# Tokens' 1/rms spread by four fp32r products with a constant square, and four weight remainders moved from GpSimd to VectorE

## The chip, the cores and the metric

The kernel runs on one core of a Trainium2 chip. The metric is the device time of one execution in microseconds, as the median of several runs. TensorE (PE) multiplies, VectorE (DVE), ScalarE (ACT) and GpSimd (POOL) work on vectors, SyncE (SP) issues most transfers.

## What is computed

One decoder layer on 1024 tokens of width 1024, in float32. Cut to what matters here:

```python
h = rmsnorm(x, norm_g) * (1 + scale) + shift      # 1/rms of every token
u = h @ w_in                                      # 40 tiles of 128 columns
cv, cg, cs, lx, ls = split(u)
v = causal_depthwise_conv(cv * sigmoid(cg))       # 31 taps
y_conv = (silu(layernorm(v)) @ pw2 + b) * silu(cs)
hs = linear_scan(a, bx)                           # from lx, gates r and i
y = concat(y_conv, hs * silu(ls)) @ w_out
out = rmsnorm(x + (1 + gate) * y, final_g)
```

`rmsnorm` multiplies by `rsqrt(mean(x * x) + 1e-6)`; `shift`, `scale` and `gate` are products of `silu(c)` with `mod_w`.

## The kernel before

Channels lie on the partitions, the 1024 tokens along the free axis, so a tile is 128x1024, and products are made in halves of 512 tokens. A float32 product is made of three products in fp32r: each operand is split into a rounded part (`hi`, a cast by ScalarE) and the remainder (`lo`, a subtraction, `SUB` at L382), and hi x hi, lo x hi and hi x lo are summed in PSUM. Three such products in a row are called a triple below.

All instructions are put into one list by a planner (`Plan`, L120). Every operation has an engine, an assumed cost, a priority (lower goes first) and the buffers that it reads and writes; `Plan.order` runs the five engines in a model of time, and an engine that is free takes the ready operation of lowest priority. What comes out is a fixed order for each engine, and each engine then executes its own order strictly. So any number in the table of constants can move instructions far from the place that it names.

The kernel begins with four tiles of `w_in`, `FIRST` (L32): for every group k of 128 channels, x is scaled by `gs` and split (`uh`, `ul`), and their products are summed in seven banks of PSUM (`first`, `fw_mm`, L796). The eighth half has no bank and is made afterwards (`late`, L1340). These products do not yet hold 1/rms or shift: 1/rms, one value per token and the same on all partitions (`rbc`), is multiplied in when they leave PSUM (`first_u`, L1336 and L1344), and the share of shift is added as a bias. That bias is a product of `shift` with the weights: `fsum` collects it on VectorE (L973 to L1006), and the product `psbias` (L1009) sums it over the partitions. The three tiles of `NEXT` (numbers 4, 5 and 6) are made in the same way, from number 7 on the finished input h is used, which takes the place of `uh` and `ul` (`inputs`, L1026).

The statistics for 1/rms: ScalarE squares x, VectorE sums the squares of the eight groups into `sq` (L933 to L943), so that 128 partial sums per token are left. Eight products with a column of ones (L949) put the sums of 128 tokens each into columns of the bank `psb`; root and reciprocal work on 128x8 values (`st`); one product turns them into 8 rows of 128 (`turn`, L959); these are copied out, written to DRAM and read back on all 128 partitions (L962 to L966). `psb` is also the name `token_stats` in the profile.

The remainders `lo` of the weights are made by GpSimd for the tiles with a number below `EARLY` = 11, and by VectorE from there on (`weights`, L494). `p_prep` is the priority of cast and remainder. `conv_tile` makes the 31 taps; for three of the tiles, with partial sums that GpSimd's queue adds by DMA. All convolutions are summed in `csum`, whose mean over the channels is a product with the constant square `minus_r` (-1/1024 everywhere, L440), and so is the sum of squares behind it (`root_by_ones`, L1277): a cast, a remainder, two products for each half, and then a reciprocal root with one Newton step. This is the same construction that the change uses for 1/rms.

Of the kernel before, what the change touches and what calls it, by code (L numbers as in the profile page):

```python
# [9 lines left out]
F32 = mybir.dt.float32  # L10
# [4 lines left out]
P = 128  # L15
# [69 lines left out]
GLO = 'DVE'  # L85
GDOT = 'DVE'
FOLD = 'DVE'
EARLY = 11
ISSUE, FLIGHT, RATE = 1.0, 10.0, 3.0
GM = 14  # L90
TAPP = 15
TP = -60
SCALE = ("DVE", "DVE", "DVE", "DVE", "DVE", "DVE", "DVE", "DVE")
SQP, RSP, BIP, HHP, HCH, EVP = -84, -110, -50, -56, 0.1, -80
RBC_LAG = 2.0
FIRSTCOST, EARLYRATE, SQD, SQK, ULS = {-99: 1.7, -98: 0.9, -97: 1.0, -96: 1.6}, 410e3, 1, 1, 1.2


# [21 lines left out]
class Plan:  # L120
# [14 lines left out]
    @staticmethod  # L135
    def keys(items):
        for it in items:
            if isinstance(it, tuple):
                yield it
            else:  # L140
                for i in range(it.parts):
                    yield (it, i)
# [162 lines left out]
def hymba_layer(ctx: ExitStack, tc: tile.TileContext, xT, xa, vecs, mod_w, mod_s0, w_first, w_pairs, w_in,  # L305
# [76 lines left out]
    def SUB(prio, eng, lo, full, hi, n=T, r=(), w=(), reserve=0):  # L382
        return TT(prio, eng, lo, full, lambda: hi().bitcast(F32), ALU.subtract, n, r, w, reserve)
# [8 lines left out]
    def DMA(prio, out, in_, nbytes, r=(), w=(), after=(), reserve=0):  # L392
        cost = max(0.1, nbytes / (EARLYRATE if prio < -94.5 + KT * 3.3 else 360e3))
        cost = FIRSTCOST.get(round(prio), cost) if prio < -94 else cost
        return S.op("SP", cost, lambda: sp.dma_start(out(), in_()), prio, r, w, after=after,
                    reserve=reserve)
# [7 lines left out]
    def big_buf(name, dt=F32, parts=1):  # L404
        return S.buf("big", name, dt, parts)
# [39 lines left out]
    def ctile(name, n):  # L445
        return const.tile([P, n], F32, tag=name, name=name)
# [30 lines left out]
    def w_slice(s, k, nk, p_load, p_prep, first_load=(), eng="POOL", late=()):  # L477
        n, c = nk * P, slice(k, k + nk)
        keys = lambda b: [(b, i) for i in range(k, k + nk)]
        rw, hi, lo = raw[s], whi[s], wlo[s]  # L480
        cut = lambda b: (lambda: k3(b)()[:, c, :])
        DMA(p_load, cut(rw), lambda: wsrc(s)[:, c, :], n * P * 4, w=keys(rw), after=first_load)
        ACT(p_prep, cut(hi), cut(rw), "copy", n, r=keys(rw), w=keys(hi), after=late)
        SUB(p_prep, eng, cut(lo), cut(rw), cut(hi), n, r=keys(rw) + keys(hi), w=keys(lo))

    def w_bufs(s, where=None):
        n = number[s]
# [5 lines left out]

    def weights(s, after=(), n=None, eng=None, where=None, late=()):  # L494
        n = number[s] if n is None else n
        eng = eng or ("POOL" if n < EARLY else "DVE")
        w_bufs(s, where)
        w_slice(s, 0, KT, n - 2.5, n - 1.4, after, eng, late)

# [20 lines left out]
    def half(b, i):  # L520
        return part(b, i * H, i * H + H)
# [224 lines left out]
    cs, ps_c = ctile("cs", KT), [bank(f"c_row{z}") for z in range(len(CPARTS))]  # L746
    ps_g, cd = bank("scale0"), CPARTS[-1][0]
    ACT(-130, lambda: cs, lambda: V[:, OFF["c"]:OFF["c"] + KT], AF.Silu, KT, w=[("cs", 0)])
    ACT(-101, lambda: junk, lambda: eps_t, AF.Sqrt, 1, r=[("cs", 0)], w=[("junk", 0)])

    def idle_mm():
        pe.matmul(psb()[:, :P], ones, ones, start=True, stop=True)
# [180 lines left out]
    sqs = []  # L933
    for k in range(KT):
        p = SQP + k
        sq = big_buf(f"sq{k}")
        ACT(p, sq, xt[k], AF.Square, r=[xt[k]], w=[sq], after=[scaled[k]])
        if k:
            to = sqs[0]
            TT(p, SUM[k], to, to, sq, ALU.add, r=[to, sq], w=[to],  # L940
               after=[last_split[k + SQD]] if k <= SQK else [])
        else:
            sqs.append(sq)  # L943
    rbc = big_buf("rbc", parts=4)
    st, wk = ctile("st", KT), [psb]

    def stats(sq, k):
        for b in range(KT):
            pe.matmul(psb()[:, b:b + 1], sq()[:, b * P:b * P + P], ones[:, 0:1],  # L949
                      start=k == 0 and b == 0, stop=k == len(sqs) - 1, skip_group_check=True)  # L950

    for k, sq in enumerate(sqs):
        S.op("PE", 0.23 * KT, lambda sq=sq, k=k: stats(sq, k), RSP, [sq], wk, columns=4 * P * KT,
             after=[last_u[LASTK - 1, 3, 0]] if k else [])
    root = ACT(RSP, lambda: st, lambda: psb()[:, :KT], AF.Sqrt, KT, bias=eps_t,
               scale=1.0 / D, r=wk, w=[("st", 0)])
    S.op("DVE", 0.2, lambda: dve.reciprocal(st, st), RSP, [("st", 0)], [("st", 0)])

    def turn():  # L959
        pe.matmul(psb()[:KT, P:2 * P], st, ident, start=True, stop=True)  # L960
    spread = S.op("PE", 0.2, turn, RSP, [("st", 0)], wk, columns=4 * P)
    row, flat = lambda: rbc()[:KT, :P], dram.tile([KT, P], F32, tag="rrow", name="rrowd")  # L962
    spread_out = ACT(RSP, row, lambda: psb()[:KT, P:2 * P], "copy", P, r=wk, w=[(rbc, 0)])
    S.op("ACT", 0.3, lambda: act.dma_start(flat, row()), RSP, [(rbc, 0)], [("rrowd", 0)], lag=0.1)
    DMA(RSP, rbc, lambda: flat.rearrange("b p -> (b p)").partition_broadcast(P), FULL_BYTES,
        r=[("rrowd", 0)], w=[rbc])  # L966


    fsum, bias = big_buf("fsum", parts=2), ctile("bias", len(FIRST + NEXT))
    facc = part(fsum, 0, FW)  # L970
    for s in NEXT:
        weights(s, where="all", late=[root if s == NEXT[0] else spread_out])
    for k in range(KT):  # L973
        p = due[f"h{k}"]
        a_ = col(macc, k)
# [87 lines left out]
    def apart(b, a, e):  # L1063
        return lambda: b().rearrange("p (q m) -> p q m", q=2)[:, :, a // 2:e // 2]
# [262 lines left out]
    for i, (s, ps) in enumerate(zip(FIRST, psf)):  # L1327
        j, p, bi = s[1] % KT, EVP + i, bias[:, i:i + 1]
        t = big_buf(f"first_u{i}", parts=4)
        for a, e in START:  # L1330
            tk, pk, n = halves(t, a, e), halves(ps, a, e), e - a
            if (a, e) in cuts[i]:
                alone = len(cuts[i]) == 1
                if alone:
                    ACT(RSP, part(t, a, e), part(ps, a, e), "copy", n, r=pk, w=tk)
                TT(p - 4 * alone, "DVE", part(t, a, e), part(t if alone else ps, a, e),  # L1336
                   part(rbc, a, e), ALU.mult, n, r=(tk if alone else pk) + halves(rbc, a, e),
                   w=tk).slack = RBC_LAG
            else:
                late = bank("late")  # L1340
                for k in range(KT):
                    fw_mm(RSP + 60 + 0.1 * k, late, i, uhs[k], uls[k], k, ((a, e),),
                          after=[spread], off=a)
                TT(p, "DVE", part(t, a, e), part(late, 0, n), part(rbc, a, e), ALU.mult, n,  # L1344
                   r=[late] + halves(rbc, a, e), w=tk)
            if s[1] < CG:
                if a == 0:
                    v[j] = big_buf(f"v{j}")
                STT(p + 3, apart(v[j], a, e), by_two(t, a, e), bi, by_two(sig[j], a, e), ALU.add,
                    ALU.mult, n, r=tk + halves(sig[j], a, e) + [("bias", 0)], w=[v[j]])  # L1350
        if s[1] >= CG:
            ACT(p + 3, t, t, AF.Sigmoid, bias=bi, r=[t, ("bias", 0)], w=[t])
            sig[j] = t
# [303 lines left out]
```

## Time and profile before

| | |
|---|---|
| median of 3 runs | 727.97 us (727.45 to 728.03) |
| profiled execution: its time, its span | 727.49 us, 725.5 us |
| granted TensorE clock | 0.998 |
| HBM | 107 GB/s over the span |
| GpSimd's remainders `wlo<-raw,whi` | 7, of 2.39 to 3.38 us |
| VectorE's remainders of the same shape | 39, 1.22 us each |
| loads of a ScalarE table | 47, 1.28 us each |

The span goes from the first to the last instruction. A group's row in the profile names the line of the source, the engine, the operation, the tile written and the tiles read. Lines are those of the kernel before; in the changed kernel the same lines stand one or two further down.

### The profile page before, as it was taken

What the parts mean: (1) busy time and instruction counts of PE and PEld (TensorE: products, weight loads), DVE (VectorE), ACT (ScalarE), POOL (GpSimd) and SP (SyncE); (2) the same over time, 40 slices, a digit from 0 to 9 for tenths busy, and PEclk for the clock granted to TensorE, in tenths of its full rate; (3) what the DMA queues carried; (4) which work ended last, traced back from release to release, by engine and by line L of the source; (5) the groups of instructions that cost most, each with busy time, mean ns of one, the idle gap of its engine ahead of it and who ended that gap; (6) DMA issues with size and microseconds to landing.
All of it is one profiled execution on the core that took longest, in us unless ns stands there. A gap on an engine that the chain in (4) does not pass through costs nothing.

```text
span 725.5 us, 8895 instructions
## 1 busy us (share of the span) xinstructions
PE 717.6 (99%) x3250; PEld 597.2 (82%) x3250; DVE 634.4 (87%) x898; ACT 469.9 (65%) x653; POOL 97.5 (13%) x105
## 2 busy tenths in 40 slices
PE   9999999999999999999999999999999999999996
PEld 7888888888888888888888888888888888888886
DVE  6978999999989987787899995998999766997757
ACT  7663766777877878947758885835764334645443
POOL 0042013121232332232021100000000000000001
PEclk9999999999999999999999999999999999999999
DMA  8971026588699799698784545243332530434216
GB/s 334 407 265 63 1 94 136 137 190 190 144 254 239 152 222 221 144 204 169 175 172 101 111 88 161 88 174 134 127 117 77 212 116 2 159 111 137 60 57 232
DMA packets 36634, 112.10 MB, mean 155 GB/s; under 512 B 4072, under 2 KB 10992, under 8 KB 36592
## 3 DMA queue, kind: packets, MB, share of 16 engines
q1 hardware_dynamic: 23760, 76.89, 29.8%
q0 software_dynamic: 12528, 34.26, 26.2%
q8 instruction: 25, 0.41, 0.2%
q10 hardware_dynamic: 304, 0.40, 0.2%
q14 instruction: 17, 0.14, 0.1%
HBM read 64.69 MB, written 12.59 MB: 107 GB/s over the span
## 4 chain that ended last, share of the span: by engine, by line
PE 99%; DVE 0%; ACT 0%; DVEq 0%; issue 0%
PE ps L506 66%; PE first L805 5%; PE pbpw L617 3%; PE pupw L617 3%; PE papw L617 3%; PE gate L1246 3%; PE out L687 2%; PE puout L617 2%; PE paout L617 2%; PE pcpw L617 1%; PE pb0out L617 1%; PE pcout L617 1%; PE late L805 1%; PE out6b L687 1%; PE c_row L757 0%; PE pb1out L617 0%
## 5 line engine op out<-in xcount | busy, mean ns | idle before, releaser
L506 PE MATMUL ps<-uh,whi 128*128 128x512 f32 x576 | 224.2, 389 | 0.0
L506 PE MATMUL ps<-ul,whi 128*128 128x512 f32 x576 | 224.2, 389 | 0.0
L506 PE MATMUL ps<-uh,wlo 128*128 128x512 f32 x576 | 224.2, 389 | 0.0
L506 PEld LDWEIGHTS ps<-uh,wlo 128*128 128x128 f32 x576 | 108.1, 188 | 22.5
L506 PEld LDWEIGHTS ps<-ul,whi 128*128 128x128 f32 x576 | 108.1, 188 | 22.4
L506 PEld LDWEIGHTS ps<-uh,whi 128*128 128x128 f32 x576 | 108.1, 188 | 22.3
L347 ACT CAST whi<-raw 128x1024 fp32r<-128x1024 f32 x46 | 47.9, 1046 | 35.7 <-PE ps L506 30.4
L355 ACT ACT_TABLE_LOAD x47 | 60.3, 1283 | 5.5 <-PE ps L506 3.4
L374 DVE TENSOR_TENSOR wlo<-raw,whi 128x1024 fp32r<-128x1024 f32 x39 | 47.5, 1218 | 17.2 <-ACT whi L347 17.1
L379 POOL DMA_DIRECT2D es<-cq x45 | 39.6, 894 | 152.5 <-ACT cq L355 84.9
L366 DVE SCALAR_TENSOR_TENSOR cacc<-v,V,cacc 128x511 f32<-128x511 f32 (+14 forms) x75 | 55.5, 740 | 0.5
L366 DVE SCALAR_TENSOR_TENSOR caccs<-v,V,caccs 128x511 f32<-128x511 f32 (+6 forms) x70 | 52.1, 744 | 1.4
L366 DVE SCALAR_TENSOR_TENSOR caccs<-c,wsum,caccs 128x511 f32<-128x511 f32 (+6 forms) x70 | 51.9, 741 | 0.6
L379 POOL DMA_DIRECT2D oo<-co x42 | 39.9, 949 | 90.9 <-ACT co L355 61.3
L506 PE MATMUL ps<-yh,wlo 128*128 128x512 f32 x128 | 49.8, 389 | 0.0
L506 PE MATMUL ps<-yh,whi 128*128 128x512 f32 x128 | 49.8, 389 | 0.0
L506 PE MATMUL ps<-yl,whi 128*128 128x512 f32 x128 | 49.8, 389 | 0.0
L374 POOL TENSOR_TENSOR fg<-fg,bc 128x512 f32<-128x512 f32 x2 | 2.5, 1280 | 281.5 <-ACT bc L347 281.5
L366 DVE SCALAR_TENSOR_TENSOR xs<-ps,V,xs 128x512 f32<-128x512 f32 (+3 forms) x48 | 35.7, 743 | 0.2
L355 ACT ACTIVATE cq<-v,V 128x511 f32<-128x511 f32 (+14 forms) x45 | 31.7, 710 | 0.0
L366 DVE SCALAR_TENSOR_TENSOR modw<-modw,sc 128x1024 f32<-128x1024 f32 x23 | 30.1, 1313 | 0.4 <-DMA modw<-in_mod_w_dram 0.4
L355 ACT ACTIVATE cq<-c,wsum 128x512 f32<-128x512 f32 x42 | 29.9, 714 | 0.0
(385 smaller groups left out, 1444.7 us busy)
## 6 DMA issues: line engine op xcount, KB each, us to landing
raw<-in_w_in_dram SPq DMA_DIRECT2D x36, 512.0 KB, 5.2
modw<-in_mod_w_dram SPq DMA_DIRECT2D x23, 512.0 KB, 9.1
raw<-in_w_out_dram SPq DMA_DIRECT2D x10, 512.0 KB, 3.6
scsd<-scs SPq DMA_DIRECT2D x8, 512.0 KB, 3.8
acc<-in_xT_dram SPq DMA_DIRECT2D x8, 512.0 KB, 4.6
accd<-acc SPq DMA_DIRECT2D x8, 512.0 KB, 2.6
rawpw<-in_pw_dram SPq DMA_DIRECT2D x8, 512.0 KB, 3.3
scsr<-scsd SPq DMA_DIRECT2D x8, 512.0 KB, 6.1
```

Source lines behind the costliest of these rows:

```text
L347: act.copy(out(), in_())
L355: act.activation(out=out(), in_=in_(), func=func, **kw)
L366: dve.scalar_tensor_tensor(out=out(), in0=in0(), scalar=scalar, in1=in1(), op0=op0, op1=op1, accum_out=accum)
L374: lambda: e.tensor_tensor(out=out(), in0=a(), in1=b(), op=op), prio, r, w,
L379: return S.op("POOL", ISSUE, lambda: pool.dma_start(out(), a(), accum_op=ALU.add), prio, r, w, lag=RATE * n / T, after=after)
L506: pe.matmul(part(ps, a - off, b - off)(), k3(lhs)()[:, k, :], rhs[k]()[:, a:b], start=(k == 0 and lhs is wh and rhs is xh and (a - off) % ...
L617: pe.matmul(part(ps, 0, c1 - c0)(), half(*lhs)()[:, j * P:j * P + P], half(*rhs)()[:, c0:c1], start=start and j == 0 and z == 0, stop=j == ...
L687: pe.matmul(part(ps, a - off, e - off)(), k3(lhs)()[:, k, :], rhs()[:, i * H + a % H:i * H + a % H + e - a], start=k == KORD[0] and lhs is ...
L805: pe.matmul(part(ps, a - off, b - off)(), fw_part(lhs, k, i * P, i * P + P)(), rhs()[:, a:b], start=k == 0 and lhs is wh and rhs is xh, st ...
L1246: pe.matmul(ps(), lhs()[:, j, :], rhs()[:, c0:c1], start=st == 0, stop=st == 2)
```

## The change

The statistics are made in another way, in two halves of 512 tokens. ScalarE rounds the sum of squares to fp32r and VectorE takes the remainder (`sqhl`); two products with `minus_r` leave the negative mean of squares of every token on all 128 partitions; ScalarE copies it out of PSUM. Then ScalarE takes the reciprocal root (`Abs_reciprocal_sqrt`) and half of its square (`sqq`), and VectorE makes a Newton step of two operations that ends in `rbc`. The products with ones, the turning product, the reciprocal on 128x8 and the way over DRAM go. The table that ScalarE loads at the start is that of the reciprocal root.

The remainders of the weights with the numbers 4 to 7 are made by VectorE, each at a priority of its own (`LOP`). The casts of the `NEXT` weights no longer wait for the statistics. The table `VL` moves the multiplication that makes `v` of the first convolution tile far back, and `RBC_LAG`, an assumed wait of the planner, is 0.

```diff
-EARLY = 11
+EARLY, VL = 11, (28, 3)
+
+LOP = {4: -112, 5: -76.2, 6: -73.2, 7: -57}
...
-RBC_LAG = 2.0
+RBC_LAG = 0.0
...
-        SUB(p_prep, eng, cut(lo), cut(rw), cut(hi), n, r=keys(rw) + keys(hi), w=keys(lo))
+        SUB(LOP.get(p_load + 2.5, p_prep), eng, cut(lo), cut(rw), cut(hi), n, r=keys(rw) + keys(hi), w=keys(lo))
...
-        eng = eng or ("POOL" if n < EARLY else "DVE")
+        eng = eng or ("POOL" if n < EARLY and n not in LOP else "DVE")
...
-    ACT(-101, lambda: junk, lambda: eps_t, AF.Sqrt, 1, r=[("cs", 0)], w=[("junk", 0)])
+    ACT(-101, lambda: junk, lambda: eps_t, AF.Abs_reciprocal_sqrt, 1, r=[("cs", 0)], w=[("junk", 0)])
...
-        sq = big_buf(f"sq{k}")
+        sq = big_buf(f"sq{k}", parts=1 if k else 2)
...
-    st, wk = ctile("st", KT), [psb]
-
-    def stats(sq, k):
-        for b in range(KT):
-            pe.matmul(psb()[:, b:b + 1], sq()[:, b * P:b * P + P], ones[:, 0:1],
-                      start=k == 0 and b == 0, stop=k == len(sqs) - 1, skip_group_check=True)
-
-    for k, sq in enumerate(sqs):
-        S.op("PE", 0.23 * KT, lambda sq=sq, k=k: stats(sq, k), RSP, [sq], wk, columns=4 * P * KT,
-             after=[last_u[LASTK - 1, 3, 0]] if k else [])
-    root = ACT(RSP, lambda: st, lambda: psb()[:, :KT], AF.Sqrt, KT, bias=eps_t,
-               scale=1.0 / D, r=wk, w=[("st", 0)])
-    S.op("DVE", 0.2, lambda: dve.reciprocal(st, st), RSP, [("st", 0)], [("st", 0)])
-
-    def turn():
-        pe.matmul(psb()[:KT, P:2 * P], st, ident, start=True, stop=True)
-    spread = S.op("PE", 0.2, turn, RSP, [("st", 0)], wk, columns=4 * P)
-    row, flat = lambda: rbc()[:KT, :P], dram.tile([KT, P], F32, tag="rrow", name="rrowd")
-    spread_out = ACT(RSP, row, lambda: psb()[:KT, P:2 * P], "copy", P, r=wk, w=[(rbc, 0)])
-    S.op("ACT", 0.3, lambda: act.dma_start(flat, row()), RSP, [(rbc, 0)], [("rrowd", 0)], lag=0.1)
-    DMA(RSP, rbc, lambda: flat.rearrange("b p -> (b p)").partition_broadcast(P), FULL_BYTES,
-        r=[("rrowd", 0)], w=[rbc])
+    wk, total = [psb], sqs[0]
+
+    both, sqh, roots = big_buf("sqhl", F32R, 2), big_buf("sqq", parts=2), []
+    for z, (a, e) in enumerate(FULL):
+        tk, hk, rk = halves(total, a, e), halves(sqh, a, e), halves(rbc, a, e)
+        ACT(RSP, half(both, 0), part(total, a, e), "copy", H, r=tk, w=[(both, 0)])
+        SUB(RSP, "DVE", half(both, 1), part(total, a, e), half(both, 0), H, r=[*tk, (both, 0)], w=[(both, 1)])
+
+        def sums():
+            for i in range(2):
+                pe.matmul(psb()[:, :H], minus_r, half(both, i)(), start=i == 0, stop=i == 1, skip_group_check=True)
+        spread = S.op("PE", 2 * (H + 32) / 2400, sums, RSP, [(both, 0), (both, 1)], wk, columns=2 * H)
+        ACT(RSP, part(total, a, e), lambda: psb()[:, :H], "copy", H, r=wk, w=tk)
+        roots.append((tk, hk, rk, a, e))
+    for tk, hk, rk, a, e in roots:
+        root = ACT(RSP, part(rbc, a, e), part(total, a, e), AF.Abs_reciprocal_sqrt, H, bias=eps_t, scale=-1.0,
+                   r=tk, w=rk)
+        ACT(RSP, part(sqh, a, e), part(rbc, a, e), AF.Square, H, scale=0.5 ** 0.5, r=rk, w=hk)
+        STT(RSP, part(total, a, e), part(total, a, e), -EPS, part(sqh, a, e), ALU.add, ALU.mult, H, r=tk + hk, w=tk)
+        STT(RSP, part(rbc, a, e), part(total, a, e), 1.5, part(rbc, a, e), ALU.add, ALU.mult, H,
+            r=tk + rk, w=rk)
...
-        weights(s, where="all", late=[root if s == NEXT[0] else spread_out])
+        weights(s, where="all")
...
-                STT(p + 3, apart(v[j], a, e), by_two(t, a, e), bi, by_two(sig[j], a, e), ALU.add,
+                STT(p + VL[j], apart(v[j], a, e), by_two(t, a, e), bi, by_two(sig[j], a, e), ALU.add,
```

What it moves shows in the engines' orders. First TensorE, at the end of the `first` products: `token_stats` is the bank `psb`, each row is one product (or several), with the tile written, the moving and the constant tile read, and the size written. Before:

```order
L949 MATMUL token_stats<-ones,sq_188 128x1 x8
L805 MATMUL first_1_202<-uh_458,fhi_349 128x512
L805 MATMUL first_1_202<-uh_458,flo_369 128x512
L805 MATMUL first_1_202<-ul_471,fhi_349 128x512
L805 MATMUL first_0_173<-uh_458,fhi_349 128x512
L805 MATMUL first_0_173<-uh_458,flo_369 128x512
L805 MATMUL first_0_173<-ul_471,fhi_349 128x512
L805 MATMUL first_1_204<-uh_458,fhi_349 128x512
L805 MATMUL first_1_204<-uh_458,flo_369 128x512
L805 MATMUL first_1_204<-ul_471,fhi_349 128x512
L960 MATMUL token_stats<-ident,st 8x128
```

The same place in the change:

```order
L957 MATMUL token_stats<-sqhl,minus_r 128x512 x2
L807 MATMUL first_1_202<-uh_456,fhi_347 128x512
L807 MATMUL first_1_202<-uh_456,flo_367 128x512
L807 MATMUL first_1_202<-ul_469,fhi_347 128x512
L807 MATMUL first_0_177<-uh_456,fhi_347 128x512
L807 MATMUL first_0_177<-uh_456,flo_367 128x512
L807 MATMUL first_0_177<-ul_469,fhi_347 128x512
L807 MATMUL first_1_205<-uh_456,fhi_347 128x512
L807 MATMUL first_1_205<-uh_456,flo_367 128x512
L807 MATMUL first_1_205<-ul_469,fhi_347 128x512
L957 MATMUL token_stats<-sqhl,minus_r 128x512 x2
```

The first pair stands two triples later than the eight products with ones did, three triples lie between the pairs, and behind the second pair `late` begins at once, where two triples stood between the turning product and `late` before.

Then VectorE at the same time, from the last `modw` rows (the products of `silu(c)` with `mod_w`) to the first evacuation `first_u`. Before:

```order
L366 SCALAR_TENSOR_TENSOR modw_397,macc<-modw_397,sc 128x1024
L957 RECIPROCAL st<-st 128x8
L366 SCALAR_TENSOR_TENSOR fsum<-fraw_131,shift,fsum 128x512
L977 TENSOR_TENSOR shift<-macc,V 128x1
L366 SCALAR_TENSOR_TENSOR fsum<-fraw_192,shift,fsum 128x512
L366 SCALAR_TENSOR_TENSOR modw_406,macc<-modw_406,sc 128x1024
L374 TENSOR_TENSOR first_u_491<-late,rbc 128x512
L374 TENSOR_TENSOR first_u_602<-first_0_171,rbc 128x512
```

In the change:

```order
L376 TENSOR_TENSOR sqhl<-sq_186,sqhl 128x512
L978 TENSOR_TENSOR shift<-macc,V 128x1 x2
L368 SCALAR_TENSOR_TENSOR modw_404,macc<-modw_404,sc 128x1024
L368 SCALAR_TENSOR_TENSOR fsum<-fraw_129,shift,fsum 128x512
L978 TENSOR_TENSOR shift<-macc,V 128x1
L368 SCALAR_TENSOR_TENSOR fsum<-fraw_190,shift,fsum 128x512
L368 SCALAR_TENSOR_TENSOR sq_186<-sq_186,sqq 128x512
L368 SCALAR_TENSOR_TENSOR fsum<-fraw_190,shift,fsum 128x512
L376 TENSOR_TENSOR wlo_569<-raw_440,whi_556 128x1024
L368 SCALAR_TENSOR_TENSOR rbc<-sq_186,rbc 128x512
L368 SCALAR_TENSOR_TENSOR sq_186<-sq_186,sqq 128x512
L376 TENSOR_TENSOR first_u_496<-first_u_496,rbc 128x512
```

The second half remainder, the remainder of tile 4 (`wlo_569`) and three of the four Newton operations stand here now. `late` is evacuated after the other halves instead of first, and the remainders of tiles 5 and 6 stand behind it, with one row of tile 4 between them; that of tile 7 comes later still, among the rows that scale x.

Last, VectorE near the end of the linear scan of the last head (`r7`, `xs7`, `sls7`), with the buffer numbers kept; `c5` is the last convolution tile, `es5` and `oo5` its partial sums, `yl1` the remainder of the first input of the output products. Before:

```order
L374 TENSOR_TENSOR xs7_3522<-xs7_3522,r7_3745 128x1024
L374 TENSOR_TENSOR c5_2228<-c5_2228,es5_2226 128x512
L1259 SCALAR_TENSOR_TENSOR r7_3745<-a7_3773,xs7_3522 128x1024
L374 TENSOR_TENSOR c5_2228<-c5_2228,oo5_2234 128x512
L374 TENSOR_TENSOR sls7_3636<-sls7_3636,r7_3745 128x1024
L374 TENSOR_TENSOR yl1_3889<-sls1_1488,yh1_3874 128x1024
```

In the change:

```order
L376 TENSOR_TENSOR xs7_3521<-xs7_3521,r7_3749 128x1024
L1260 SCALAR_TENSOR_TENSOR r7_3749<-a7_3773,xs7_3521 128x1024
L376 TENSOR_TENSOR sls7_3635<-sls7_3635,r7_3749 128x1024
L376 TENSOR_TENSOR c5_2220<-c5_2220,es5_2218 128x512
L376 TENSOR_TENSOR yl1_3889<-sls1_1481,yh1_3878 128x1024
```

One `c5` row moved behind the scan, the other behind all seven `yl` rows. On TensorE the triple of tile 40 that reads the sixth `yl` stands one triple earlier, and the four `mean` products one triple later; from there to the end TensorE's order is the same.

## The prediction

> **What bounds the kernel now.** I read the profile's page first, then the waits of TensorE, then the chain that ended last, and at last the timeline of the two places that the change touches.
>
> ```profile
> PE 717.6 (99%) x3250; PEld 597.2 (82%) x3250; DVE 634.4 (87%) x898; ACT 469.9 (65%) x653; POOL 97.5 (13%) x105
> PE   9999999999999999999999999999999999999996
> DVE  6978999999989987787899995998999766997757
> PE 99%; DVE 0%; ACT 0%; DVEq 0%; issue 0%
> ```
>
> TensorE is busy in every slice but the last, and the chain that ended last is TensorE for 99% of the span. Its list of waits holds two entries:
>
> ```profile
> PE token_stats L752 <- DVE ones L439: 1.1, 1, 1.1
> PE first L805 <- ACT fhi L347: 0.6, 1, 0.6
> ```
>
> Both lie in the first microseconds, which the change leaves alone. So TensorE is the bound and waits for nobody afterwards: the time falls by what its own stream loses, and rises by any wait that the change makes. These pieces of the chain (start, length, line, number) price its work:
>
> ```profile
> 42.65 1.68 PE token_stats L949 x16
> 53.91 23.12 PE ps L506 x102
> 77.03 1.46 PE psbias L1011 x14
> 480.54 0.93 PE mean L1303 x4
> ```
>
> One 128x512 product is 23.12 / 102 = 0.2267 us. The `mean` row is the operation that the change adds, a sum over partitions by the constant square `minus_r`: four products, 0.93 us.
>
> **TensorE's own work.** The timeline around the old statistics (start, length):
>
> ```profile
> 39.91 1.22 DVE L374 TENSOR_TENSOR sq<-sq,sq 128x1024 f32<-128x1024 f32 x1
> 42.01 0.59 ACT L347 COPY first_u<-first 128x512 f32<-128x512 f32 x1 [2.48 <-PE first L805]
> 42.19 1.22 DVE L366 SCALAR_TENSOR_TENSOR modw<-modw,sc 128x1024 f32<-128x1024 f32 x1
> 42.26 0.39 PE L805 MATMUL first<-ul,fhi 128*128 128x512 f32 x1
> 44.19 0.49 PE L805 MATMUL first<-uh,fhi 128*128 128x512 f32 x1
> 46.78 0.51 PE L805 MATMUL first<-uh,fhi 128*128 128x512 f32 x1
> 48.29 0.39 PE L805 MATMUL late<-uh,fhi 128*128 128x512 f32 x1
> ```
>
> From the product at 42.26 to the first `late` product at 48.29 are 6.03 us. They hold that product and fifteen more of `first`, 16 x 0.2267 = 3.63 us. The other 2.40 us are the statistics (42.26 to 44.19 instead of 0.23: 1.70), and the turning product with its waits and a slow product or two (0.70). All of it goes. The four new products cost 0.93. **Term one: -1.47 us**, all on the path. `late` then starts at about 46.8.
>
> **The chain between the new products.** Each half of the tokens goes ScalarE cast, VectorE remainder, two products, ScalarE copy; the second half reuses the same bank and the same buffer, so it waits for the first. Its steps have rows in the layer norm, which does the same thing to 128x512 pieces:
>
> ```profile
> 504.51 1.14 ACT L347 CAST hilnss<-lnss 128x512 fp32r<-128x512 f32 x2 [0.97 <-DVE lnss L374]
> 505.53 1.29 DVE L374 TENSOR_TENSOR lolnss<-lnss,hilnss 128x512 fp32r<-128x512 f32 x2
> 507.14 1.26 ACT L355 ACTIVATE lnbc<-lnss,eps_t 128x512 f32<-128x512 f32 x2 [0.19 <-PE lnss L1286]
> 508.29 1.15 ACT L355 ACTIVATE qlnss<-lnbc 128x512 f32<-128x512 f32 x2
> 509.64 1.28 DVE L366 SCALAR_TENSOR_TENSOR lnss<-lnss,qlnss 128x512 f32<-128x512 f32 x2
> ```
>
> First half: the sum of squares is whole at 41.1, the cast done at 41.8; VectorE, which began a `modw` row at 42.19, now takes the remainder there and ends it at 42.9. TensorE, two triples later than before, is there at 43.9: one microsecond to spare. Second half: the last product of the first half issues at about 44.1; ScalarE starts 0.43 after an issue (the copy at 42.01 follows the `first` product three before the one at 42.26), copy 0.48 until the next starts, cast 0.6, remainder 0.7, two hand-overs of some 0.05: ready at 46.4. TensorE, after nine more `first` products and the first of its pair, asks at 44.1 + 0.23 + 9 x 0.2267 + 0.23 = 46.6. **0.2 us to spare**; I count nothing, and at most 0.5 (a copy more) should a step be slower.
>
> After that 1/rms is ready on all partitions at about 54.4 by the same rows (ScalarE: `whi` of tile 7 and `fsum` among the copy, root and square; VectorE: the four combinations, with the first remainder between them). Before, its first reader started at 53.95. So the first evacuations are no earlier, but the banks are not missed: TensorE wants the first of them for the second half of tile 4 at 46.8 + 2 x 5.44 = 57.7, the first evacuation ends at 55.1. The remainder of tile 4 is placed after its cast, done at 50.6 on ScalarE, and ends at 51.9; TensorE reads it at 52.7. Cost nothing; if that cast is late by more than 0.8, the excess is lost.
>
> **VectorE up to the bias product.** This is the tight place. `psbias` stands after 102 products of tiles 4 to 6 and reads `fsum`, the last link of all the shift work on VectorE:
>
> ```profile
> 45.65 13.36 POOL L374 TENSOR_TENSOR wlo<-raw,whi 128x1024 fp32r<-128x1024 f32 x5 [44.34 <-ACT whi L347]
> 46.26 3.42 DVE L366 SCALAR_TENSOR_TENSOR modw<-modw,sc 128x1024 f32<-128x1024 f32 x1
> ...
> 53.95 0.69 DVE L374 TENSOR_TENSOR first_u<-late,rbc 128x512 f32<-128x512 f32 x1 [4.27 <-PE late L805]
> 54.56 3.67 DVE L374 TENSOR_TENSOR first_u<-first,rbc 128x512 f32<-128x512 f32 x6
> 58.15 1.42 DVE L374 TENSOR_TENSOR first_u<-first_u,rbc 128x512 f32<-128x512 f32 x1
> 64.83 0.69 DVE L374 TENSOR_TENSOR next<-ps,rbc 128x512 f32<-128x512 f32 x1 [1.39 <-PE ps L506]
> 70.27 0.69 DVE L374 TENSOR_TENSOR next<-ps,rbc 128x512 f32<-128x512 f32 x1 [0.34 <-PE ps L506]
> 75.71 0.69 DVE L374 TENSOR_TENSOR next<-ps,rbc 128x512 f32<-128x512 f32 x1
> 76.32 0.28 DVE L374 TENSOR_TENSOR fsum<-raw 128x128 f32<-128x128 f32 x1
> ...
> 76.87 1.62 PE L1011 MATMUL psbias<-ones,fsum 128*128 128x1 f32 x14
> ```
>
> VectorE ends `fsum` at 76.60, TensorE asks at 76.87: 0.27 to spare. What VectorE gains before that: the idle 4.27 + 1.39 + 0.34 = 6.0, and two stretched rows. `modw` takes 3.42 beside GpSimd's remainders where 1.22 is usual (2.2), and the seventh evacuation 1.42 where its like takes 0.68 (0.74). Those remainders leave GpSimd: 8.9 us in all. What it takes on: three remainders (tile 7's comes later), two half remainders, four combinations, less a small reciprocal.
>
> ```profile
> L374 DVE TENSOR_TENSOR wlo<-raw,whi 128x1024 fp32r<-128x1024 f32 x39 | 47.5, 1218 | 17.2 <-ACT whi L347 17.1
> L374 POOL TENSOR_TENSOR wlo<-raw,whi x7: 2393/2409/3382, 45.6 to 111.6; 128x1024 fp32r<-128x1024 f32 x7
> ```
>
> That is 3 x 1.15 (1.22 with the overlap of successive rows off) + 1.29 + 2 x 1.28 - 0.1 = 7.2 us. New waits for ScalarE, for the second cast (0.45) and the first `fsum` (0.35), make 0.8. VectorE is thus 8.9 - 7.2 - 0.8 = 0.9 us earlier, while TensorE is 1.47 earlier: 0.57 less room. Against it stand the 0.27 above and the 0.2 that VectorE waited at 75.71 for TensorE. **Term two: +0.1 us**, between 0 and 0.8 (any row of the ledger may be a few tenths out).
>
> The stretched rows deserve a second reading, since they carry 2.9 us of the ledger. GpSimd's 2.4 us remainder and VectorE's two-input rows each wait for the other to end: 3.42 is 1.15 plus about the length of one. [...]
>
> **Behind that.**
>
> ```profile
> 40.00:60.00 20.00, 20.00 (x97) 16.38 (x96) 15.69 (x25) 12.18 (x25) 13.36 (x5) 1.00 0.54 196
> ```
>
> Four remainders leave GpSimd, which is busy 13.36 us of this window; what it keeps is not waited for sooner. ScalarE trades a 128x8 root, an 8x128 copy and a transfer issue for two casts, two copies, two roots and two squares, some 4 us more, where the window from 40 to 60 (after the clocked span, its columns are TensorE, weight loads, VectorE, ScalarE, GpSimd) has it busy for 12.18 of 20; it loads the root table where it loaded the square root's, and no table more. The broadcast of 1/rms to 128 partitions is gone from SP's queue, so the loads behind it come sooner and nobody waits for them. From tile 7 on, VectorE has one remainder more, but evacuates `v` of tile 0 after the inputs instead of before, 2 x 0.68 the other way: even. The longer convolution sums move by fractions within a stretch where TensorE waits for none of them. The last place with another order is at 460 to 480:
>
> ```profile
> 464.49 0.67 DVE L374 TENSOR_TENSOR c<-c,oo 128x512 f32<-128x512 f32 x1
> 466.21 8.03 DVE L374 TENSOR_TENSOR yl<-sls,yh 128x1024 fp32r<-128x1024 f32 x7
> 479.00 1.23 DVE L374 TENSOR_TENSOR meanl<-csum,meanh 128x1024 fp32r<-128x1024 f32 x1 [1.11 <-ACT meanh L347]
> ```
>
> The sixth `yl` ends at 466.21 + 6 x 1.15 = 473.1. Counted back 29 products from `mean` at 480.54, TensorE reads it at 473.97; now three products sooner, 0.68. VectorE has one `c` row of 0.6 less ahead of it, so 0.8 us of room stay. `meanl` ends at 480.23, read at 480.77; `mean` is now three products later, so room grows. Both count as nothing. The tail has the same order as before and moves with TensorE.
>
> **Sum.** -1.47 + 0.1 = -1.4 us. The profiled execution took 727.49 (span 725.5 and 2.0 around it), so 726.1 by it; it lies 0.48 below the median of the runs, 727.97, so I predict 727.97 - 1.4 = **726.6**.
>
> **Rivals.** *Late VectorE* (0.22): the ledger is short by half a microsecond to 1.5, `psbias` waits, and the gain is mostly eaten: 727.4. For it: the spare 0.2; against: TensorE's bound held everywhere in the old order. *VectorE's surplus goes to TensorE* (0.10, slower): if the stretched rows do not shrink, or new ones arise beside the remainders that GpSimd keeps, VectorE is 2.9 us later than in the ledger; `psbias` and then the inputs of tile 7 wait, 726.6 + 2.9 = 729.5. The change is slower than before once VectorE loses over 1.4 us beyond the ledger. Against it: after 55 GpSimd has one remainder there instead of five. *The second pair is not hidden* (0.08): the products on the constant square wait for copy, cast and remainder, up to 0.5 and as much again in what follows: 727.3, so the change would not do what it says. Otherwise the forecast (0.57), 726.3 to 727.0, and 0.03 for a gain still larger.
>
> **Numbers.** What a measurement can tell here is about 0.2%, 1.46 us, so the border of faster is 726.5, inside the forecast's own spread: of its 0.57 I give 0.36 to faster. Faster 0.39, same 0.51, slower 0.10. The range takes in the bounds of both terms and the first and third rival: 726.0 to 728.8.
>
> **What would show it.** Right: no wait of TensorE between 42 and 715; `late` at 46.8 instead of 48.29; `psbias` at 75.4; VectorE's `modw` rows all near 1.2; `yl` still read without a gap. Wrong: an idle entry of `psbias` on `fsum`, of `token_stats` on `sqhl`, or of a tile's `wlo` product; a cadence of products other than 0.2267.

## The result and the profile after

| | time, median of runs | against the kernel before, 95% interval |
|---|---|---|
| before | 727.73 us (16 runs) | |
| after | 726.29 us (725.55 to 726.75, 16 runs) | 0.9977 (0.9970 to 0.9985) |
| after, measured again | 725.94 us (11 runs; before 727.73, 28 runs) | 0.9975 (0.9966 to 0.9984) |

The change saves 1.4 to 1.8 us, about 0.2%. The profiled execution of the changed kernel took 726.39 us (span 724.4). From its page the engines, TensorE in 40 slices and the shares of the chain, then its whole list of waits of TensorE:

```profile
PE 717.0 (99%) x3236; PEld 596.9 (82%) x3236; DVE 638.9 (88%) x907; ACT 474.2 (65%) x659; POOL 86.6 (12%) x101
PE   9999999999999999999999999999999999999996
PE 99%; DVE 0%; ACT 0%; issue 0%; DVEq 0%
```

```profile
PE token_stats L754 <- DVE ones L441: 1.1, 1, 1.1
PE first L807 <- ACT fhi L349: 0.5, 1, 0.5
```

Nothing new waits: TensorE is the bound as before, and its two waits lie in the first microseconds. It has 14 matrix instructions fewer: 16 of the old sums and 2 of the turn gone, 4 come. GpSimd lost its four rows and 11 us. VectorE gained 4.5 against this profile of the old kernel, but 1.1 against a second one (637.8), so that its own total says little. The chain, in order of time (start, length, line, number):

```profile
8.36 36.33 PE first L807 x159
44.69 0.47 PE token_stats L957 x2
45.15 2.07 PE first L807 x9
47.22 0.46 PE token_stats L957 x2
47.69 5.44 PE late L807 x24
53.13 23.12 PE ps L508 x102
...
557.12 2.72 PE papw L619 x12
```

The old statistics and their turn (1.68 + 0.32 in the chain) are now two pieces of 0.47 and 0.46. This execution began its first tile product at 8.36, the one before at 7.71, so times have to be counted from there: `late` stood at 48.45 - 7.71 = 40.74 us and stands at 47.69 - 8.36 = 39.33, **1.41 us earlier**; the first pointwise projection (`papw`) at 550.18, now 548.76, **1.42 earlier**. What is won at the statistics is still there 500 us later, whole. The timeline of the places that the prediction called narrow:

```profile
46.33 0.69 DVE L376 TENSOR_TENSOR sqhl<-sq,sqhl 128x512 fp32r<-128x512 f32 x1 [1.01 <-ACT sqhl L349]
47.06 0.63 PE L957 MATMUL token_stats<-sqhl,minus_r 128*128 128x512 f32 x2
51.23 1.22 DVE L376 TENSOR_TENSOR wlo<-raw,whi 128x1024 fp32r<-128x1024 f32 x1
54.17 0.69 DVE L368 SCALAR_TENSOR_TENSOR rbc<-sq,rbc 128x512 f32<-128x512 f32 x1
54.78 3.67 DVE L376 TENSOR_TENSOR first_u<-first,rbc 128x512 f32<-128x512 f32 x6
55.66 2.40 POOL L376 TENSOR_TENSOR wlo<-raw,whi 128x1024 fp32r<-128x1024 f32 x1 [54.36 <-ACT whi L349]
74.93 0.69 DVE L376 TENSOR_TENSOR next<-ps,rbc 128x512 f32<-128x512 f32 x1
75.53 0.28 DVE L376 TENSOR_TENSOR fsum<-raw 128x128 f32<-128x128 f32 x1
76.09 1.62 PE L1012 MATMUL psbias<-ones,fsum 128*128 128x1 f32 x14
```

The second remainder of the sums ends at 47.02, 0.04 before its pair begins and 0.27 before the product that reads it. The remainder of tile 4 ends at 52.45, the last 1/rms at 54.86, and GpSimd's one remainder (2.40 us, where the shortest of its like took 2.39) beside the six evacuations (0.61 each, where the rows just ahead follow one another by 0.60) lengthens neither.

### The profile page after: what moved, and what is told of

The parts are those of the page before. It is cut to its first block, busy times and chain, and to the rows that moved or that the text cites. A ratio compares the mean times of both kernels' runs of the same rounds, so it can differ in the third digit from the quotient of the medians.

```text
span 724.4 us, 8887 instructions
## 1 busy us (share of the span) xinstructions
PE 717.0 (99%) x3236; PEld 596.9 (82%) x3236; DVE 638.9 (88%) x907; ACT 474.2 (65%) x659; POOL 86.6 (12%) x101
## 4 chain that ended last, share of the span: by engine, by line
PE 99%; DVE 0%; ACT 0%; issue 0%; DVEq 0%
PE ps L508 66%; PE first L807 5%; PE pupw L619 3%; PE papw L619 3%; PE gate L1247 3%; PE pbpw L619 3%; PE out L689 2%; PE puout L619 2%; PE paout L619 2%; PE pcpw L619 2%; PE pb0out L619 1%; PE pcout L619 1%; PE late L807 1%; PE out6b L689 1%; PE c_row L759 1%; PE pb1out L619 0%
## 5 line engine op out<-in xcount | busy, mean ns | idle before, releaser
L508 PE MATMUL ps<-uh,whi 128*128 128x512 f32 x576 | 224.2, 389 | 0.0
L508 PE MATMUL ps<-ul,whi 128*128 128x512 f32 x576 | 224.1, 389 | 0.0
L508 PE MATMUL ps<-uh,wlo 128*128 128x512 f32 x576 | 224.1, 389 | 0.0
L508 PEld LDWEIGHTS ps<-uh,wlo 128*128 128x128 f32 x576 | 108.1, 188 | 22.5
L508 PEld LDWEIGHTS ps<-ul,whi 128*128 128x128 f32 x576 | 108.1, 188 | 22.4
L508 PEld LDWEIGHTS ps<-uh,whi 128*128 128x128 f32 x576 | 108.1, 188 | 22.3
L376 DVE TENSOR_TENSOR wlo<-raw,whi 128x1024 fp32r<-128x1024 f32 x43 | 52.5, 1221 | 17.0 <-ACT whi L349 16.7
L368 DVE SCALAR_TENSOR_TENSOR cacc<-v,V,cacc 128x511 f32<-128x511 f32 (+14 forms) x75 | 55.8, 744 | 0.4
L508 PE MATMUL ps<-yh,wlo 128*128 128x512 f32 x128 | 49.8, 389 | 0.0
L508 PE MATMUL ps<-yl,whi 128*128 128x512 f32 x128 | 49.8, 389 | 0.0
L508 PE MATMUL ps<-yh,whi 128*128 128x512 f32 x128 | 49.8, 389 | 0.0
L357 ACT ACTIVATE co<-v,V 128x511 f32<-128x511 f32 (+13 forms) x42 | 29.4, 708 | 0.0
```

Source lines behind the costliest of these rows:

```text
L357: act.activation(out=out(), in_=in_(), func=func, **kw)
L368: dve.scalar_tensor_tensor(out=out(), in0=in0(), scalar=scalar, in1=in1(), op0=op0, op1=op1, accum_out=accum)
L376: lambda: e.tensor_tensor(out=out(), in0=a(), in1=b(), op=op), prio, r, w,
L508: pe.matmul(part(ps, a - off, b - off)(), k3(lhs)()[:, k, :], rhs[k]()[:, a:b], start=(k == 0 and lhs is wh and rhs is xh and (a - off) % ...
```

## The experiments

Each of the twelve was measured beside runs of the kernel before on the same chip. For each, three stretches are read from the chain, because the start moves from one execution to the next: the start of the first tile product, from there to `papw` (the body), and from the end of the last product to the end of the last instruction in the trace (the close).

| kernel | median, us | ratio to before (95%) | start | body | close |
|---|---|---|---|---|---|
| before | 727.73 | | 7.71 | 550.18 | 6.15 |
| before again | 727.53 | 0.9996 (0.9988 to 1.0005) | 7.64 | 550.16 | 6.14 |
| after | 726.29 | 0.9977 (0.9970 to 0.9985) | 8.36 | 548.76 | 5.83 |
| after again | 725.94 | 0.9975 (0.9966 to 0.9984) | 8.10 | 548.76 | 5.83 |
| remainders moved only | 726.82 | 0.9988 (0.9980 to 0.9997) | 7.58 | 550.17 | 5.71 |
| sums twice | 726.40 | 0.9984 (0.9976 to 0.9993) | 8.27 | 549.71 | 5.83 |
| sums five times | 729.57 | 1.0028 (1.0017 to 1.0039) | 7.30 | 552.53 | 5.83 |
| one VectorE row more | 726.01 | 0.9980 (0.9971 to 0.9990) | 7.32 | 549.01 | 5.83 |
| two VectorE rows more | 727.14 | 0.9994 (0.9984 to 1.0003) | 7.47 | 550.14 | 5.84 |
| v of tile 0 put back | 725.48 | 0.9973 (0.9964 to 0.9982) | 7.60 | 548.84 | 5.85 |
| one product each, statistics | 725.73 | 0.9975 (0.9966 to 0.9984) | 7.56 | 548.33 | 5.83 |
| one product each, everywhere | 724.54 | 0.9959 (0.9946 to 0.9971) | 7.55 | 547.35 | 5.84 |

From `papw` to the last product it is 161.40 to 161.45 us in all of these.

### Both kernels again

> The changed kernel once more, beside the others on one chip: 1.4 us below the kernel before. In the profile before it the first product of a tile began 0.65 us later than in that of the kernel before, in the others 0.1 to 0.4 earlier. Theory (that start moves by itself from run to run): here it begins at another time, somewhere in 7.3 to 8.4, and from it to the first product of the pointwise projections are 548.8 us again. Rival (the change makes the start later): 8.3 again.

> The kernel before once more, for a second profile: ratio 1. From the first product of a tile to the first of the pointwise projections 550.2 us as before, and the start somewhere in 7.3 to 8.4. From the last product's end to the end of the span it showed 6.1 us where four other kernels show 5.8; if that is a matter of chance, it is between the two here.

The bodies repeat to 0.02 us, so that small differences can be read from one profile of each, which medians with a spread of 1 us don't show. The start was 8.10, between the two guesses; the other kernels with the same head began at 7.30 to 8.27, and those with the old head at 7.58 to 7.71. So it moves by itself by up to a microsecond, and the changed kernel is not bound to a late one. The close is no chance, though: 6.14 and 6.15 with the old kernel, 5.71 to 5.85 with every other in the table. More on it below.

### Where the gain comes from

The remainders alone, with the old statistics (the kernel before, and of the diff these two lines and their use):

```diff
+LOP = {4: -112, 5: -76.2, 6: -73.2, 7: -57}
-        eng = eng or ("POOL" if n < EARLY else "DVE")
+        eng = eng or ("POOL" if n < EARLY and n not in LOP else "DVE")
```

> The moved remainders alone, with the old statistics. Theory: TensorE's stream is the same and waits for nobody, so the time is that of the kernel before, 0 within 0.4 us, though VectorE's stretched modw row shrinks from 3.42 to 1.22 us. Rival (the gain comes from GpSimd's remainders that no longer block VectorE): 1 to 1.4 us below the kernel before.

The body is that of before to 0.01 us, with the theory; VectorE's rows beside the moved remainders are short, in its timeline:

```profile
47.51 1.22 DVE L368 SCALAR_TENSOR_TENSOR modw<-modw,sc 128x1024 f32<-128x1024 f32 x1
48.05 2.94 POOL L376 TENSOR_TENSOR wlo<-raw,whi 128x1024 fp32r<-128x1024 f32 x1 [46.74 <-ACT whi L349]
```

The `modw` row that took 3.42 before takes 1.22, and that is worth nothing, since TensorE waited for none of it. Yet the time fell by 0.78 (from 727.60 beside it), more than the 0.4 allowed: 0.44 of it is the close, which neither theory had, and about 0.1 the start; the rest shows in no profile and lies within the spread of the runs.

The new products made twice, and five times:

```diff
-            for i in range(2):
+            for i in (0, 1) * 5:
                 pe.matmul(psb()[:, :H], minus_r, half(both, i)(), start=i == 0, stop=i == 1, ...)
```

> The changed kernel with each pair of the new products made twice into the same bank, so four products more and the sums doubled (the result is scaled by it). Theory: the stream of TensorE is the bound there, 4 x 0.2267 = 0.91 us more than the changed kernel, 0.5 us below the kernel before. Rival (the products fill time in which TensorE would wait for the chain of cast, remainder and copy): 0 to 0.4 us more than the changed kernel.

> The changed kernel with each pair of the new products made five times into the same bank (each pair starts the sum anew, so the result is the same): sixteen products more. Theory (TensorE's stream is the bound there): 16 x 0.2267 = 3.63 us above the changed kernel, between 3.4 and 3.8, 2.2 above the kernel before. Rival (part of the products fill time in which TensorE would wait for the chain of cast, remainder and copy): under 3.0 above the changed kernel.

(In the first of the two the expectation had the sums doubled; each pair starts the sum anew, so they are not.) The body grows by 0.95 for four products and by 3.77 for sixteen: 0.236 each, against 0.2267 reckoned. The medians say 3.63 for sixteen, and only 0.1 to 0.5 for four, which the movement of the start can hide; the larger dose settles it. Every product there is paid in full, and none fills a wait.

The other direction: leave the remainder's product out in the statistics, then in the layer norm's mean and sums too.

```diff
-        SUB(RSP, "DVE", half(both, 1), part(total, a, e), half(both, 0), H, ...)
-            for i in range(2):
-                pe.matmul(psb()[:, :H], minus_r, half(both, i)(), start=i == 0, stop=i == 1, ...)
+            pe.matmul(psb()[:, :H], minus_r, half(both, 0)(), start=True, stop=True, ...)
```

> The changed kernel with one product for each half of the tokens: the remainder of the sum of squares is left out of the statistics, two products and two VectorE half rows fewer. Theory (TensorE's stream): 2 x 0.2267 = 0.45 us below the changed kernel, 2.2 below the kernel before. Rival (the chain between the two halves is the limit there): 0.

> As the one before, and the remainders of the layer norm's mean and of its two sums of squares left out too: six products fewer than in the changed kernel. Theory (TensorE's stream): 6 x 0.2267 = 1.36 us below the changed kernel, 3.1 below the kernel before. Rival (the products of the layer norm stand in a place where their inputs come late): 0.45, as the one before.

Bodies 0.43 and 1.41 below the changed kernel, against 0.45 and 1.36: TensorE's stream again, also in the layer norm. The last of them is the fastest of all, 724.54 us, at the price of sums whose rounding remainder is dropped.

### Is VectorE up to the bias product the tight place?

One more row, and two, hidden from the planner's costs so that no order changes up to the bias product:

```diff
+    spare = big_buf("spare")
+    S.op("DVE", 0.0, lambda: dve.tensor_tensor(out=spare(), in0=xt[0](), in1=xt[1](), op=ALU.mult),
+         -73.1, [xt[0], xt[1], (wlo[NEXT[2]], 0)], [spare])
```

> The changed kernel with one more two-input 128x1024 row on VectorE (1.15 us, its result is read by nobody), between the remainder of tile 6 and the end of fsum; nothing else in the order up to the bias product changes. Theory (VectorE up to the bias product is the tight place, 0.28 us ahead of TensorE and twice 0.2 us idle for it): psbias waits 0.4 to 0.7 us for fsum, the time is 0.5 us above the changed kernel. Rival (VectorE has room there): 0, no wait of psbias. Other rival (the lateness of VectorE also reaches the inputs of tile 7): 1.1 us or more.

> The changed kernel with two more two-input 128x1024 rows on VectorE (2.30 us) between the remainder of tile 6 and the end of fsum. With one such row the bias products waited for nothing, and TensorE lost 0.2 us at a ul of tile 7 at 90. Theory (the room is 0.3 us of VectorE's own idle time and 0.6 us ahead of the inputs of tile 7, and what exceeds it goes to TensorE whole): 1.15 us more than with one row, 1.4 above the changed kernel (1.2 to 1.6), the waits at the inputs of tile 7 or at psbias. Rival (there is more room at the inputs, and the 0.2 was a slip): 0.5 or less above the changed kernel.

With one row the body grew by 0.25, half of the 0.5 forecast, and not where it was forecast: 0.20 of it is a stop at an input of tile 7, at 90.6. In the timeline of that kernel:

```profile
75.06 1.62 PE L1015 MATMUL psbias<-ones,fsum 128*128 128x1 f32 x14
75.30 0.28 DVE L376 TENSOR_TENSOR fsum<-raw 128x128 f32<-128x128 f32 x1
...
90.55 0.19 PEld L508 LDWEIGHTS ps<-ul,whi 128*128 128x128 f32 x1 [0.34 <-DVE ul L368]
```

`psbias` begins while the last piece of `fsum` is not even started. Its fourteen instructions are seven columns of the bias, each of which reads 128 columns of `fsum`, and only the last two read the last piece. With two rows that shows directly, in the timeline and in the waits:

```profile
75.19 1.39 PE L1016 MATMUL psbias<-ones,fsum 128*128 128x1 f32 x12
76.56 0.27 DVE L376 TENSOR_TENSOR fsum<-raw 128x128 f32<-128x128 f32 x1
76.89 0.38 PE L1016 MATMUL psbias<-ones,fsum 128*128 128x1 f32 x2 [0.30 <-DVE fsum L376]
...
91.81 0.19 PEld L508 LDWEIGHTS ps<-ul,whi 128*128 128x128 f32 x1 [0.66 <-DVE ul L368]
```

```profile
PE psbias L1016 <- DVE fsum L376: 0.3, 1, 0.3
PE ps L508 <- DVE ul L368: 0.2, 1, 0.2
```

Twelve go, the last two wait. Counted from product start to product start, TensorE loses 0.44 there and 0.29 and 0.50 at two inputs of tile 7, 1.23 together; the body is 1.38 longer and the median 1.20, as the theory had it (1.2 to 1.6). Here a wait reads as 0.2 in the list and costs half a microsecond: the weight load waits 0.66, and the product after a stop takes 0.11 longer.

What the change did to `v` of tile 0, undone:

```diff
-EARLY, VL = 11, (28, 3)
+EARLY, VL = 11, (3, 3)
```

> The changed kernel with the evacuation of v of tile 0 put back ahead of the inputs of tile 7. Theory (the extra rows showed 0.6 us of room ahead of those inputs, and two rows of 0.68 ahead of them take 1.2): TensorE waits 0.4 to 0.9 us at a ul of tile 7, 0.6 above the changed kernel. Rival (it is a place with room): 0.

A miss: the body is 548.84, and no `ul` is waited for. The planner also moved products of TensorE there (those of tile 8, from the second half of tile 6 on), so this doesn't measure the room; it shows only that the later `v` is not needed for the gain. The median is 0.5 below that of the changed kernel, with an earlier start and the same body, so not a faster kernel by anything the profile shows.

### What the moved remainders are for

The new statistics with all of tiles 4 to 7 back on GpSimd, then with tile 4's alone on VectorE:

```diff
-LOP = {4: -112, 5: -76.2, 6: -73.2, 7: -57}
+LOP = {}
```

> The new statistics alone; the remainders of tiles 4 to 7 stay on GpSimd. Theory (TensorE's own stream carries the gain, and the move only keeps it): TensorE loses its 1.47 us around the statistics, but GpSimd makes the remainder of tile 4 last of three (2.4 us each, and each lengthened by a two-input row of VectorE), so TensorE waits for it at about 52: 1.5 us, between 0.5 and 3. Time within 0.3 us of the kernel before, or up to 1.5 above it. Rival (the move of the remainders does nothing for the time): as the changed kernel, 1.4 us below the kernel before, with no wait for wlo.

```diff
+LOP = {4: -112}
```

> The changed kernel with only the remainder of tile 4 on VectorE, those of tiles 5 to 8 on GpSimd. With all of them on GpSimd it was 14 us slower than the changed kernel: 3.6 at the late remainder of tile 4 (a wait of 1.8 and nine products at a lower rate behind it), 2 at the inputs of tile 7, the rest in the layer norm. Theory (two separate costs: tile 4's remainder, and VectorE's rows that GpSimd blocks): no wait for wlo and no slow products at 54, but VectorE's two-input rows still take 2 to 3.4 us, and TensorE still waits 1 to 2.5 us at the inputs of tile 7, so 1 to 3 us above the changed kernel ahead of the layer norm. Rival (the late remainder of tile 4 was all): ahead of the layer norm within 0.3 us of the changed kernel.

740.30 us, 1.0175 (1.0161 to 1.0189), and 740.76, 1.0184 (1.0170 to 1.0198): **13 us slower than the kernel before**, where the first theory allowed 1.5. Its mechanism is there, the wait for the remainder of tile 4, but it was a small part. The timeline of the first:

```profile
49.13 8.13 POOL L376 TENSOR_TENSOR wlo<-raw,whi 128x1024 fp32r<-128x1024 f32 x3 [0.24 <-ACT whi L349]
49.61 2.64 DVE L368 SCALAR_TENSOR_TENSOR sq<-sq,sqq 128x512 f32<-128x512 f32 x1 [0.18 <-ACT sqq L357]
52.28 2.73 DVE L368 SCALAR_TENSOR_TENSOR rbc<-sq,rbc 128x512 f32<-128x512 f32 x1
54.52 0.50 PE L508 MATMUL ps<-uh,wlo 128*128 128x512 f32 x1 [1.79 <-POOL wlo L376]
```

GpSimd makes remainders of 2.4 us in 2.7, and three of the combinations for 1/rms, two-input rows of 0.69, take 2.64, 2.73 and 2.08 beside them. Then a window table of the same kernel (stretch, its length and TensorE, weight loads, VectorE, ScalarE, GpSimd, granted clock, transfers):

```profile
50.00:54.50 4.50, 2.73 (x13) 1.92 (x11) 4.47 (x2) 4.48 (x8) 4.50 (x3) 1.00 0.96 375
54.50:55.80 1.30, 1.28 (x6) 1.06 (x7) 1.20 (x3) 1.29 (x4) 1.30 (x1) 1.00 0.70 287
55.80:59.20 3.40, 3.40 (x10) 2.66 (x9) 3.40 (x4) 1.55 (x5) 2.72 (x2) 0.50 0.00 0
59.20:62.00 2.80, 2.80 (x14) 2.32 (x13) 2.77 (x3) 0.99 (x3) 1.45 (x1) 1.00 0.00 0
```

TensorE waits for the remainder, at a stretch of 2.0 us between two products. It starts again at the full clock, but from 55.8 to 59.2 the granted clock is 0.50, and products come every 0.427 us instead of 0.227. That is another 1.6 us for a wait of 1.8. The half clock began 1.3 us after the pause had ended (54.5) and lasted 3.4 us. A second pause of the same length, at 91.4 for a `ul` of tile 7, brought no slow stretch: the granted clock is 1.00 from 80 to 100.

With tile 4's remainder on VectorE the stop for `wlo` shrinks to 0.3 us, nearly gone as expected, but two of the combinations still take 2.92 and 2.77 us beside GpSimd, the evacuations come late, and TensorE finds no free bank. Its waits, and a window of it:

```profile
PE ps L508 <- DVE first_u L376: 2.8, 1, 2.8
```

```profile
62.00:64.40 2.40, 2.40 (x7) 1.86 (x6) 2.40 (x5) 0.00 (x0) 0.00 (x0) 0.50 0.00 0
```

Again the clock halves behind it. Added up from product start to product start, waits and slow products ahead of the layer norm are 5.8 us in the first kernel and 5.2 in the second, against 1 to 3 expected of the second. Both mechanisms were rightly named; the price was too small by the slow clock and by the banks. The rest of the loss, 9.1 us in the first kernel and 10.0 in the second, lies at 568 to 588, where TensorE waits for the layer norm's outputs, in pieces of up to 1.0 us and at half clock again (0.52 at 571 to 576). In both kernels the layer norm's mean stands at 499 us instead of 480. The chain of the first, beside that of the changed kernel's line `506.77 50.35 PE ps L508 x222`, shows why that costs so much:

```profile
499.08 0.93 PE mean L1304 x4
525.88 0.93 PE lnss L1287 x4
```

TensorE's order is another one there. In both kernels 60 products more stand ahead of `mean` than in the changed kernel, and behind `lnss` 156 products are left until the pointwise projections instead of 222, that is 66 x 0.2267 = 15.0 us less work while the layer norm's outputs are made. GpSimd, the fifth pair of the window row, does nothing meanwhile:

```profile
571.00:576.00 5.00, 4.40 (x8) 2.05 (x8) 5.00 (x7) 1.96 (x3) 0.00 (x0) 0.52 0.11 45
```

So these 9 to 10 us come with the order that the planner chose for these two kernels, and not from rows that block each other there; why it chose that order was not traced, and no run put the remainders back and kept the order. Ahead of the layer norm TensorE's order differs too, though less: `psbias` stands 24 and 18 products later.

## Why the prediction was right, and where it was not

**TensorE as the bound: right.** No new wait between 42 and 715, and products added to the statistics, or taken away there and in the layer norm, were paid or won at 0.22 to 0.24 us each.

**Term one, -1.47: right, measured -1.41** at `late`. The four products cost 0.93 as the `mean` row had priced them (0.47 + 0.46), and sixteen more cost 3.77.

**The chain between the products: right.** It was to have 0.2 us of room for the second half and had 0.27; 1/rms was ready at 54.86 in an execution that started 0.65 later (54.4 predicted), and the remainder of tile 4 had 1.0 us to its product (52.45 against 53.42 in the timeline) where 0.8 were reckoned.

**The tight place: the step that failed.** The prediction set the end of `fsum` against the beginning of `psbias` and found 0.27 us. Only its last two instructions need that end: 12 x 0.112 = 1.34 us later, so the room was about 1.6. What binds first are the inputs of tile 7, right behind `fsum` on VectorE, with some 0.6 us: a row of 1.15 cost 0.25, after two pauses of VectorE's own had taken up 0.34 of it. The prediction named those inputs only in a rival. The ledger was also at least 0.5 too cautious: VectorE was to end `fsum` 0.9 earlier, and ended it at 75.53 + 0.28 - 8.36 = 67.45 after the first product instead of 68.89, 1.44 earlier. That end is set by TensorE: VectorE stood still for 0.2 us ahead of the last `next` row at 74.93, until its product was done. So **term two was 0 instead of +0.1**, and of the 0.8 that it allowed nothing came. The rival of a late VectorE was priced at the right rate (two rows more: 1.2 us), but it begins about half a microsecond later than was said.

**The blocked rows: right**, and they are more than a detail. In the changed kernel all `modw` rows take 1.22 (one took 3.42 before); GpSimd's remainder of tile 8 (2.40 us) beside six evacuations from PSUM (0.61 each) costs neither anything; with the remainders back, two-input rows of 0.69 take 2.08 to 2.92. The mechanism of the second rival, GpSimd's rows reaching TensorE through VectorE, is real and large, and the change avoids it by moving those four remainders: alone the move is worth nothing in the body, and without it TensorE loses 5.8 us ahead of the layer norm, the slow clock included. The rest of the 13 us that the new statistics lose without it comes with another order of TensorE's products.

**Behind that, all zero: right for the body**, -1.41 at `late` and -1.42 at `papw`, and with `v` put back 548.84.

**What the prediction did not have** is the close, 0.31 us shorter. The measured gain is thus -1.42 - 0.31 = -1.73 when both start alike; the second measurement's medians say -1.79, the first's -1.44. That the latter agrees so well with the -1.4 on record is in part chance: a term missed on one side, and starts that ran late on the other (8.36 in the profiled one).

## What to carry to other kernels

Where one engine is busy 99% of the time, price a change by the instructions that it takes from that engine's stream, and check everything else only for whether it makes it wait. A wait on a group of instructions ends at the one that reads the last piece: look which of them needs it before calling a place tight. And where work is shared with an engine that blocks another's rows, moving it can be worth little alone (here the 0.44 us of the close) and yet keep the rest of the change from waits that would eat it up (here 5.8 us): try each part by itself, and look whether the order of the other engines stayed the same.

## What the runs showed of the hardware

**A short pause can cost twice.** Pauses of 2.0 and 2.9 us of TensorE were followed by 3.2 to 3.4 us at half the granted clock (0.50 from 55.8 to 59.2 in the kernel with all remainders on GpSimd, from 61.2 to 64.4 in that with tile 4's alone on VectorE); another of 2.0 us (1.00 from 80 to 100 in the first of them) and those up to 0.5 us (0.998 over the whole kernel with two VectorE rows more) were not. Pauses of up to 1.0 us close behind one another, from 568 us on in the two kernels with remainders back on GpSimd, were followed by half clock too: in the first kernel 10.2 us of it (0.52 over 571 to 576 and 0.55 over 576 to 582), in the second 0.7 over the slice from 573 to 592. Why one pause of 2.0 us was followed by it and the other was not, no run shows.

**The number of GpSimd's instructions shows at the end of the program.** The close differs in GpSimd's closing instructions (drains, semaphores). Worked out from the trace's records of that engine, counting every one of its instructions from the program's start:

```
kernel                          GpSimd instructions   pause behind number   close
before, before again            199, 199              196, 196              6.15, 6.14
remainders back on GpSimd       202                   196                   6.20
tile 4's alone on VectorE       201                   196                   6.26
all the others                  190 to 193            none                  5.71 to 5.85
```

The pause is 0.32 to 0.38 us where 0.03 to 0.07 is usual, and the instruction behind it, where it is a drain, takes 0.15 longer. It stands behind the same number wherever the stream is that long, once ahead of one drain, once of another, once between two semaphores. So it goes with the length of the stream, and the four remainders fewer on GpSimd are worth 0.31 to 0.44 us here; no run changed the length by other instructions. What the pause is, no run shows: in the four profiles with it the transfer table lists an instruction transfer within 0.3 us of the span's end, and in the others none there, but in that of the kernel before it begins 0.71 us after the pause has ended.
